# Evacuations of the second group ahead of the norm's broadcast, four plus four low parts on another engine, and one evacuation queued behind the scaling of x, in a gated retention and attention layer

## Chip, cores and metric

The kernel runs on one core of one Trainium2 chip. The metric is device time in microseconds of one execution. The engines are TensorE (PE in the profile, its weight loads PEld), VectorE (DVE), ScalarE (ACT), GpSimd (POOL) and SyncE (SP, which issues the loads).

## The reference

One decoder layer over 256 tokens of width 1024, all in float32. One input projection feeds a retention branch and an attention branch; two gates merge them.

```
def hybrid_layer(x, ln_w, w_in, ret_gn_w, w_ret_o, w_moba_o, w_out):
    h = rmsnorm(x, ln_w)
    proj = jnp.einsum('bsd,de->bse', h, w_in)
    ...
    rq, rk, rv, rg, mq, mk, mv, mg, gr, gm = jnp.split(proj, splits, axis=-1)
    ret = retention(split_heads(rq, RET_HEADS), split_heads(rk, RET_HEADS), split_heads(rv, RET_HEADS))
    ret = head_groupnorm(ret, ret_gn_w).astype(x.dtype) * jax.nn.silu(rg)
    ret = jnp.einsum('bsv,vd->bsd', ret, w_ret_o)
    mo = moba_attention(split_heads(mq, MOBA_HEADS), split_heads(mk, MOBA_HEADS), split_heads(mv, MOBA_HEADS))
    mo = merge_heads(mo) * jax.nn.silu(mg)
    mo = jnp.einsum('bsv,vd->bsd', mo, w_moba_o)
    y = jax.nn.sigmoid(gr) * ret + jax.nn.sigmoid(gm) * mo
    return x + jnp.einsum('bsd,de->bse', y, w_out)
```

A final `rmsnorm` follows. Retention has 4 heads with keys of 128 and values of 256, in two chunks of 128 tokens; the change touches only the first groups of the projection, which feed it.

## The kernel before

Every float32 operand of a product is split into a high part, rounded to the type `float32r`, and a low part, the rest; a product is high times high plus the two mixed terms. A split is one copy on ACT (the high part) and one subtraction on DVE or POOL (the low part).

The weights come in 24 groups of 512 columns, and a group in 4 chunks of 512 KB (`load`, SP's queue, 6 buffers `raw`). `split` (L108, L109) makes `wh` on ACT and `wl` on DVE, 8 buffers each. `stream(g, i)` splits two chunks of group g + 1 and loads two of group g + 2, so the weights run one to two groups ahead. A load waits until DVE has read its `raw` buffer for `wl`.

Groups 0 and 1 are the retention values. They are multiplied with x that the norm has not scaled yet (`x0`, `proj_first`), and the norm's factor `rs` is applied when the two result tiles of a group are evacuated (`evac_n`: `vh` on ACT, L442, and `vl` on DVE, L444). Behind group 1 `x_stats_t` multiplies `rs` with a matrix of ones, which broadcasts it to `rsb` (copied on DVE, L194), and `norm_x(k)` scales the eight slices of x for all later groups: `z` on DVE (L163), the high part of `xs` on ACT (L164), the low part on DVE (L165).

Group 2 (retention queries, `qT`) still multiplies with `x0` and is scaled by `rsb` afterwards (L413). Group 3 (retention keys, `kT`) is the first that needs `xs`. A group of this kind makes four result tiles f = 0 to 3 (`proj_t`), each evacuated by `evac_t`: ACT copies one half, DVE adds the other (`halves`, L392 and L394), and `split_to` makes the high part on ACT (L257) and the low part on POOL (L258). The low parts of the queries are the tile `rqs`, those of the keys lie in `early`. The scores of head 0 (L252 to L254, then L316) stand between groups 3 and 4 in PE's order, and its value product (L336 to L338) between tiles f = 1 and f = 2 of group 4.

The result tiles of all projections share a pool of 4 PSUM buffers (`ps_m`). Groups 0 and 1 use all four; group 2's f = 2 and f = 3 take those of group 1's t = 0 and t = 1, and group 3's f takes that of group 2's f. A tile can begin only when DVE has finished reading the tile before it in its buffer. Each engine works through its own list in order. A scheduler makes the lists when the kernel is built, from the order of the code and its own estimates, so a line moved in the code moves in several lists.

Of the kernel before, what the change touches and what calls it, by code (L numbers as in the profile page):

```python
# [12 lines left out]


# [2 lines left out]

# [6 lines left out]
F32 = mybir.dt.float32  # L24
# [24 lines left out]
def hybrid_kernel(ctx: ExitStack, tc, xT, x, w_in, gn_w, w_ret_o, w_moba_o, w_out, fn_w, decay, out):  # L49
# [110 lines left out]
    def norm_x(k):  # L160
        xk, h, l = xt[:, KT + k * S:KT + (k + 1) * S], xs[:, k, 0], xs[:, k, 1]
        z = wk.tile([P, S], F32, name="z", tag="z", bufs=4)
        nc.vector.scalar_tensor_tensor(z, xk, lnw[:, k:k + 1], rsb, op0=ALU.mult, op1=ALU.mult)  # L163
        nc.scalar.activation(h, z, AF.Copy)  # L164
        nc.vector.tensor_sub(l, z, h.bitcast(F32))  # L165

    def rsqrt(y, a, tmp):

# [28 lines left out]
    def proj_first(g, pair):  # L197

        for k in range(KT):
            for cs in cut(g, k):  # L200
                h, l = (w[g, k // 2][:, k % 2, cs] for w in (wh, wl))
                for t, ps in enumerate(pair):
                    xh, xl = (x0s(k)[:, j, t * P:(t + 1) * P] for j in range(2))
                    nc.tensor.matmul(ps[:, cs], xh, h, start=g > 0 and k == 0, stop=False)  # L204
                    nc.tensor.matmul(ps[:, cs], xh, l, start=False, stop=False)  # L205
                    last = nc.tensor.matmul(ps[:, cs], xl, h, start=False, stop=k == KT - 1)  # L206
        return last
# [45 lines left out]
        nc.tensor.matmul(ps, a[:, 0], b[:, 1], start=False, stop=False)  # L253
        nc.tensor.matmul(ps, a[:, 1], b[:, 0], start=False, stop=True)  # L254

    def split_to(out, a):
        nc.scalar.activation(out[:, 0], a, AF.Copy)  # L257
        nc.gpsimd.tensor_sub(out[:, 1], a, out[:, 0].bitcast(F32))  # L258

    def attn_scores(h):  # L260
        q, k, i = qT[h // 4], kT[h // 4], h % 4
# [125 lines left out]
    def evac_t(g, i, ps):  # L387

        f = (i + 4) if g in (7, 8, 13, 15, 17, 19, 21) else i

        def halves(out, w=1.0):
            nc.scalar.activation(out, ps[:, 1], AF.Copy, scale=w)  # L392
            if w == 1.0:
                nc.vector.tensor_add(out, ps[:, 0], out)  # L394
            else:
                nc.vector.scalar_tensor_tensor(out, ps[:, 0], w, out, op0=ALU.mult, op1=ALU.add)

        def tmp(n):
            return wk.tile([P, S], F32, name=n, tag=n, bufs=4)

        if g in (4, 7):
            q = qT[g // 7][:, i]
            halves(q, 1.0 / math.sqrt(P))
            split_to(qs[g // 7][:, i], q[:, P:])
        elif g in (5, 8):
            k = kT[g // 8][:, i]
            halves(k)
            split_to(ks[g // 8][:, i], k)
        elif g in (2, 3):
            a = (qT if g == 2 else kT)["r"][:, i]  # L410
            halves(a)
            if g == 2:
                nc.vector.tensor_mul(a, a, rsb)  # L413
            split_to((qs if g == 2 else ks)["r"][:, i], a if g == 2 else a[:, :P])
        elif g in (12, 13):
            z, sg = tmp("z"), wk.tile([P, S], F32, name="sg", tag="sg", bufs=2)
            halves(z)
            nc.scalar.activation(sg, z, AF.Sigmoid)
            nc.vector.tensor_mul(z, z, sg)
            nc.vector.tensor_mul(oT[:, f], oT[:, f], z)  # L420
        elif g in (14, 15, 16, 17):
            z = tmp("z")
            halves(z)
            if i % 2 == 0:
                gt = new_v("gt")
                G[g // 16, f], G[g // 16, f + 1] = gt[:, :S], gt[:, S:]
            nc.scalar.activation(G[g // 16, f], z, AF.Sigmoid)
        elif g in (18, 19):
            halves(A[:, f])
            nc.gpsimd.tensor_mul(A[:, f], A[:, f], G[0, f])  # L430
        elif g in (20, 21):
            z = tmp("z")
            halves(z)
            nc.vector.tensor_mul(z, z, G[1, f])
            nc.vector.tensor_add(z, z, A[:, f])
            nc.scalar.activation(yT[:, f, 0], z, AF.Copy)
            nc.vector.tensor_sub(yT[:, f, 1], z, yT[:, f, 0].bitcast(F32))

    def evac_n(g, t, ps):
        def split_v(r1=1.0):  # L440
            h, l = new_v("vh", F32R), new_v("vl", F32R)
            nc.scalar.activation(h, ps, AF.Copy, scale=r1)  # L442
            if g < 2:
                nc.vector.scalar_tensor_tensor(l, ps, r1, h.bitcast(F32), op0=ALU.mult, op1=ALU.subtract)  # L444
            else:
                nc.vector.tensor_sub(l, ps, h.bitcast(F32))
            return h, l

        if g in (6, 9):
            if t == 0:  # L450
                V["m", g // 9] = split_v()
            else:
                v1 = new_v("v1")
                nc.scalar.activation(v1, ps, AF.Copy)
                V["m", g // 9] += (v1,)
        elif g in (0, 1):
            V["r", g] = V.get(("r", g), ()) + (split_v(rs[:, t:t + 1]),)
        elif g in (10, 11):
            nc.scalar.activation(rgate[:, t, (g - 10) * GW:(g - 9) * GW], ps, AF.Copy)
# [9 lines left out]
    def unit(g, i):  # L469

        nonlocal A, yT, rgate
        if i == 0:
            if g == 10:
                rgate = ac.tile([P, NT, D], F32, name="rgate", tag="rgate")
            if g in (2, 4, 7):
                qT["r" if g == 2 else g // 7] = new_qk("qT")
            if g == 2:
                qs["r"] = ac.tile([P, 4, 2, S], F32R, name="rqs", tag="oT")
                early = ac.tile([P, KT + KT * S], F32R, name="early", tag="big8")[:, KT:]
                ks["r"], qs[0] = (early[:, c:c + D].rearrange("p (h a s) -> p h a s", a=2, s=P) for c in (0, D))  # L480
            if g == 5:
                ks[0] = ac.tile([P, 4, 2, S], F32R, name="mk0s", tag="rgate")
            if g == 7:
                qs[1] = ac.tile([P, RET_HEADS * 3 * P], F32R, name="mq1s", tag="dec")[:, :D]
                qs[1] = qs[1].rearrange("p (h a s) -> p h a s", a=2, s=P)
            if g == 8:
                ks[1] = ac.tile([P, KT + KT * S], F32R, name="mk1s", tag="big8")[:, KT:]
                ks[1] = ks[1].rearrange("p (h a s) -> p h a s", a=2, s=S)
            if g in (3, 5, 8):
                kT["r" if g == 3 else g // 8] = new_qk("kT")  # L490
            if g == 18:
                A = ac.tile([P, KT, S], F32, name="A", tag="rgate")
            if g == 20:
                yT = ac.tile([P, KT, 2, S], F32R, name="yT", tag="xs")
        if groups[g][1] == "N":
            evac_n(g, i, proj_n(g, lambda k: xs[:, k], i))
        else:
            if g == 2:
                a = x0s
            elif g < 18:  # L500
                a = lambda k: xs[:, k]
            elif g < 20:
                a = lambda k: rT[k // 2][:, k % 2]
            else:
                a = lambda k: mT[k // 4][:, k % 4]
            for f in (2 * i, 2 * i + 1):
                evac_t(g, f, proj_t(g, a, f))
# [44 lines left out]
    for g in range(2):  # L552
        for i in range(2):
            stream(g, i)
        if g == 0:
            x_stats()
            nc.sync.dma_start(dec, decay)
        pair = [pm.tile([P, GW], F32, name="ps_m", tag="m") for t in range(NT)] if g else ps0
        last = proj_first(g, pair)
        if g:  # L560
            with tc.issue_after(last.ins):
                x_stats_t()
            for k in range(KT):
                norm_x(k)
        for t in range(NT):
            evac_n(g, t, pair[t])
    for g in range(2, NG - 2):
        for i in range(2):
            u = 2 * g + i
            stream(g, i)  # L570
            if u == 38:

                xr = new_v("xr", F32R)
                ir = wk.tile([P, P], F32R, name="ir", tag="p1", bufs=2)
                nc.scalar.activation(ir, ident, AF.Copy)
                nc.scalar.activation(xr[:, :S], xn[:, 1, D - S:], AF.Copy)
                nc.vector.tensor_sub(xr[:, S:], xn[:, 1, D - S:], xr[:, :S].bitcast(F32))
            if u == 40:
                fnw = ac.tile([P, D], F32, name="fnw", tag="qk", bufs=4)
                nc.sync.dma_start(fnw, fn_w.to_broadcast([P, D]))  # L580
                nc.gpsimd.tensor_scalar_mul(fnw, fnw, 2.0)
            for f, a in extra.get(u, []):
                f(*a)
            unit(g, i)
    for c in range(4):
        split(NG - 1, c)

# [89 lines left out]
```

## Time and profile before

| | |
|---|---|
| median of 3 runs | 305.89 us (305.42 to 306.07) |
| the profiled execution's own time | 304.77 us |
| span of that execution in the trace | 302.6 us |
| PE busy, share of the span | 293.8 us, 97% |
| DVE, ACT, POOL busy | 219.7, 192.0, 41.6 us |
| granted clock of PE, mean | 0.996 of full speed |

The profiled execution is one of its own, 1.12 us under the median of the three timed ones; 2.17 us of its time lie outside the span. PE is busy nearly all the time, so what matters are the few places where it waits, and what each of them waits for.

### The profile page before, as it was taken

The numbers are of one execution on the slowest core, as the hardware profiler recorded it, in microseconds if no ns is written. First come the engines' busy times: TensorE is split into PE (matmuls) and PEld (weight loads), VectorE is DVE, ScalarE is ACT, GpSimd is POOL, SyncE is SP. The second block draws the span as 40 slices with busy tenths as digits, with TensorE's granted clock in tenths as the row PEclk, the third lists the DMA queues.
The fourth block names the chain that finished last, engine by engine and source line by source line (L and its number), as shares of the span: only waits on it lengthen the run. The fifth ranks groups of instructions, "written<-read, shape, count | busy, mean of one in ns | idle before, by whom it ended". The sixth has DMA issues, their size and how long they took to land.

```text
span 302.6 us, 4549 instructions
## 1 busy us (share of the span) xinstructions
PE 293.8 (97%) x1628; PEld 253.8 (84%) x1628; DVE 219.7 (73%) x394; ACT 192.0 (63%) x365; POOL 41.6 (14%) x44
## 2 busy tenths in 40 slices
PE   8999999999999999999999999999999999999992
PEld 5788788899888899888888888888888888888891
DVE  3869999867699695884747899557657458899342
ACT  5787777465738676675965857757847626646231
POOL 3000039621200123200000000000000245000000
PEclk9999999999999999999999999999999999999998
DMA  6999659817274462835267184484475486440011
GB/s 195 370 409 410 249 153 341 276 67 223 68 257 128 159 205 76 246 113 198 58 219 233 48 267 147 144 274 126 155 227 179 153 265 215 145 142 1 0 69 69
DMA packets 28966, 55.08 MB, mean 182 GB/s; under 512 B 1936, under 2 KB 3984, under 8 KB 28944
## 3 DMA queue, kind: packets, MB, share of 16 engines
q1 hardware_dynamic: 28624, 54.54, 54.9%
q10 hardware_dynamic: 288, 0.26, 0.2%
q8 instruction: 12, 0.20, 0.2%
q14 instruction: 10, 0.08, 0.1%
q0 software_dynamic: 32, 0.00, 0.0%
HBM read 53.75 MB, written 1.05 MB: 181 GB/s over the span
## 4 chain that ended last, share of the span: by engine, by line
PE 92%; POOL 3%; DVE 2%; ACT 1%; issue 1%; DVEq 0%; POOLq 0%; ACTq 0%
PE ps_m L232 35%; PE ps_m L233 19%; PE ps_m L219 7%; PE ps_m L217 7%; PE ps_m L218 7%; POOL rqs L258 3%; PE ps_m L205 3%; PE ps_m L204 3%; PE ps_m L206 3%; PE ps_s L117 1%; PE ps_t L284 1%; DVE z L163 1%; PE ps_s L263 1%; PE ps_o L303 1%; DVE xs L165 1%
## 5 line engine op out<-in xcount | busy, mean ns | idle before, releaser
L232 PE MATMUL ps_m<-xs,wh 128*128 128x512 f32 x352 | 123.6, 393 | 0.3 <-DVE qT L394 0.3
L109 DVE TENSOR_TENSOR wl<-raw,wh 128x1024 fp32r<-128x1024 f32 x88 | 109.3, 1266 | 11.5 <-ACT wh L108 11.3
L233 PE MATMUL ps_m<-xs,wl 128*128 128x256 f32 x352 | 98.9, 282 | 0.0
L108 ACT ACTIVATE wh<-raw 128x1024 fp32r<-128x1024 f32 x88 | 90.3, 1053 | 7.0 <-PE ps_m L219 2.4
L232 PEld LDWEIGHTS ps_m<-xs,wh 128*128 128x128 f32 x352 | 66.0, 188 | 14.0 <-issue 0.6
L233 PEld LDWEIGHTS ps_m<-xs,wl 128*128 128x128 f32 x352 | 66.5, 189 | 0.2
L217 PE MATMUL ps_m<-wh,xs 128*128 128x512 f32 x64 | 25.5, 398 | 0.0
L218 PE MATMUL ps_m<-wl,xs 128*128 128x512 f32 x64 | 25.3, 395 | 0.0
L219 PE MATMUL ps_m<-wh,xs 128*128 128x512 f32 x64 | 25.3, 395 | 0.0
L430 POOL TENSOR_TENSOR A<-A,gt 128x256 f32<-128x256 f32 x8 | 6.8, 854 | 120.1 <-DVE A L394 120.1
L232 PE MATMUL ps_m<-rT,wh 128*128 128x512 f32 x64 | 22.2, 390 | 0.0
L232 PE MATMUL ps_m<-mT,wh 128*128 128x512 f32 x64 | 22.2, 390 | 0.0
L394 DVE TENSOR_TENSOR z<-ps_m,z 128x256 f32<-128x256 f32 x32 | 13.5, 421 | 11.8 <-ACT z L392 11.7
L392 ACT ACTIVATE z<-ps_m 128x256 f32<-128x256 f32 x32 | 12.1, 379 | 13.1 <-PE ps_m L233 12.9
L233 PE MATMUL ps_m<-rT,wl 128*128 128x256 f32 x64 | 18.0, 282 | 0.0
L233 PE MATMUL ps_m<-mT,wl 128*128 128x256 f32 x64 | 18.0, 282 | 0.0
L258 POOL TENSOR_TENSOR rqs<-qT,rqs 128x256 fp32r<-128x256 f32 x4 | 9.5, 2410 | 39.4 <-ACT rqs L257 39.4
L219 PEld LDWEIGHTS ps_m<-wh,xs 128*128 128x128 f32 x64 | 12.0, 188 | 2.9
L218 PEld LDWEIGHTS ps_m<-wl,xs 128*128 128x128 f32 x64 | 12.0, 188 | 2.5
L217 PEld LDWEIGHTS ps_m<-wh,xs 128*128 128x128 f32 x64 | 12.0, 188 | 2.5
L232 PEld LDWEIGHTS ps_m<-rT,wh 128*128 128x128 f32 x64 | 12.0, 188 | 2.5
L232 PEld LDWEIGHTS ps_m<-mT,wh 128*128 128x128 f32 x64 | 12.0, 188 | 2.5
(183 smaller groups left out, 503.6 us busy)
## 6 DMA issues: line engine op xcount, KB each, us to landing
raw<-in_w_in SPq DMA_DIRECT2D x68, 512.0 KB, 4.7
raw<-in_w_ret_o SPq DMA_DIRECT2D x8, 512.0 KB, 5.5
raw<-in_w_moba_o SPq DMA_DIRECT2D x8, 512.0 KB, 5.4
raw<-in_w_out SPq DMA_DIRECT2D x8, 512.0 KB, 5.1
raw<-in_w_in SPq DMA_DIRECT2D x7, 256.0 KB, 4.8
xn<-in_x SPq DMA_DIRECT2D x2, 512.0 KB, 7.0
xt<-in_xT SPq DMA_DIRECT2D x7, 128.0 KB, 4.1
dec<-in_decay SPq DMA_DIRECT2D x1, 768.0 KB, 9.9
```

The lines of the kernel that those rows point to most:

```text
L108: nc.scalar.activation(h, r, AF.Copy)
L109: nc.vector.tensor_sub(l, r, h.bitcast(F32))
L204: nc.tensor.matmul(ps[:, cs], xh, h, start=g > 0 and k == 0, stop=False)
L205: nc.tensor.matmul(ps[:, cs], xh, l, start=False, stop=False)
L217: nc.tensor.matmul(ps, a(k)[:, 0, sl], h, start=not begun and k == 0, stop=False)
L218: nc.tensor.matmul(ps, a(k)[:, 0, sl], l, start=False, stop=False)
L219: nc.tensor.matmul(ps, a(k)[:, 1, sl], h, start=False, stop=k == KT - 1)
L232: nc.tensor.matmul(ps, h, a(k), start=k == 0, stop=False)
L233: nc.tensor.matmul(ps[:, 0], l, a(k)[:, 0], start=False, stop=k == KT - 1)
L258: nc.gpsimd.tensor_sub(out[:, 1], a, out[:, 0].bitcast(F32))
L392: nc.scalar.activation(out, ps[:, 1], AF.Copy, scale=w)
L394: nc.vector.tensor_add(out, ps[:, 0], out)
```

## The change

Three edits. In the second group, `evac_n` of both tiles stands ahead of `x_stats_t` and `norm_x` in the code; it stood behind. `split_to` takes the engine of the subtraction as an argument, and groups 2 and 3 pass DVE, which moves eight subtractions from POOL: four of 128x256 (`rqs`) and four of 128x128 (`early`, from `kT`). And the first instruction of `norm_x(3)`, the scaling of x's fourth slice on DVE, is kept as `begun`; what unit 4 (group 2's f = 0 and f = 1, with their evacuations) puts on DVE is queued behind it.

```diff
     def norm_x(k):
...
-        nc.vector.scalar_tensor_tensor(z, xk, lnw[:, k:k + 1], rsb, op0=ALU.mult, op1=ALU.mult)
+        ins = nc.vector.scalar_tensor_tensor(z, xk, lnw[:, k:k + 1], rsb, op0=ALU.mult, op1=ALU.mult)
         nc.scalar.activation(h, z, AF.Copy)
         nc.vector.tensor_sub(l, z, h.bitcast(F32))
+        return ins.ins
...
-    def split_to(out, a):
+    def split_to(out, a, eng=nc.gpsimd):
         nc.scalar.activation(out[:, 0], a, AF.Copy)
-        nc.gpsimd.tensor_sub(out[:, 1], a, out[:, 0].bitcast(F32))
+        eng.tensor_sub(out[:, 1], a, out[:, 0].bitcast(F32))
...
-            split_to((qs if g == 2 else ks)["r"][:, i], a if g == 2 else a[:, :P])
+            split_to((qs if g == 2 else ks)["r"][:, i], a if g == 2 else a[:, :P], nc.vector)
...
         last = proj_first(g, pair)
+        for t in range(NT):
+            evac_n(g, t, pair[t])
         if g:
             with tc.issue_after(last.ins):
                 x_stats_t()
-            for k in range(KT):
-                norm_x(k)
-        for t in range(NT):
-            evac_n(g, t, pair[t])
+            begun = [norm_x(k) for k in range(KT)][3]
...
-            unit(g, i)
+            with tc.issue_after(begun) if u == 4 else nullcontext():
+                unit(g, i)
```

The line numbers of the changed kernel are one higher behind the import. DVE's list from the end of group 1 to the evacuation of group 2 (`vl` low parts of the values, `z` and `xs` the norm, `wl` weights) read before:

```order
L194 COPY rsb<-ps_s 128x256
L444 SCALAR_TENSOR_TENSOR vl<-ps_m,rs,vh 128x512
L109 TENSOR_TENSOR wl<-raw,wh 128x1024
L163 SCALAR_TENSOR_TENSOR z<-xt,rsb 128x256 x3
L165 TENSOR_TENSOR xs<-z,xs 128x256 x3
L163 SCALAR_TENSOR_TENSOR z<-xt,rsb 128x256 x3
L165 TENSOR_TENSOR xs<-z,xs 128x256 x3
L163 SCALAR_TENSOR_TENSOR z<-xt,rsb 128x256 x2
L444 SCALAR_TENSOR_TENSOR vl<-ps_m,rs,vh 128x512
L109 TENSOR_TENSOR wl<-raw,wh 128x1024
L165 TENSOR_TENSOR xs<-z,xs 128x256 x2
L109 TENSOR_TENSOR wl<-raw,wh 128x1024
```

and reads now, on the same engine and at the same place:

```order
L445 SCALAR_TENSOR_TENSOR vl<-ps_m,rs,vh 128x512
L109 TENSOR_TENSOR wl<-raw,wh 128x1024
L445 SCALAR_TENSOR_TENSOR vl<-ps_m,rs,vh 128x512
L195 COPY rsb<-ps_s 128x256
L163 SCALAR_TENSOR_TENSOR z<-xt,rsb 128x256 x4
L109 TENSOR_TENSOR wl<-raw,wh 128x1024
L165 TENSOR_TENSOR xs<-z,xs 128x256 x4
L163 SCALAR_TENSOR_TENSOR z<-xt,rsb 128x256 x3
L165 TENSOR_TENSOR xs<-z,xs 128x256 x2
L163 SCALAR_TENSOR_TENSOR z<-xt,rsb 128x256
L109 TENSOR_TENSOR wl<-raw,wh 128x1024
L165 TENSOR_TENSOR xs<-z,xs 128x256 x2
```

Both `vl` stand at the front, the second no longer behind all eight `z`; the sum of instructions is the same. The first evacuation of group 2 (`qT`) follows directly behind each of the two pieces.

What follows on DVE, from that evacuation on (`rqs` and `early` are the subtractions that POOL had), reads now:

```order
L395 TENSOR_TENSOR qT<-ps_m,qT 128x256 x2
L414 TENSOR_TENSOR qT<-qT,rsb 128x256 x2
L109 TENSOR_TENSOR wl<-raw,wh 128x1024
L259 TENSOR_TENSOR rqs<-qT,rqs 128x256 x2
L109 TENSOR_TENSOR wl<-raw,wh 128x1024
L395 TENSOR_TENSOR qT<-ps_m,qT 128x256 x2
L414 TENSOR_TENSOR qT<-qT,rsb 128x256 x2
L109 TENSOR_TENSOR wl<-raw,wh 128x1024
L259 TENSOR_TENSOR rqs<-qT,rqs 128x256 x2
```

The `rqs` rows are new here and stand between two `wl`; before, the two `wl` followed each other. Later in the same list `early` stands twice behind the `wl` that follows `kT`'s first evacuations.

Before, POOL's list at that place read

```order
L258 TENSOR_TENSOR rqs<-qT,rqs 128x256 x4
L258 TENSOR_TENSOR early<-kT,early 128x128 x4
L258 TENSOR_TENSOR early<-qT,early 128x128 x4
L258 TENSOR_TENSOR mk0s<-kT,mk0s 128x256 x4
```

and the first two of these rows are gone from it now; the attention's low parts (`early` from group 4's `qT`, then `mk0s`) stay.

## Rows read from the trace of the kernel before

**Rows 1.** Waits, PE alone, whole run: waiter, releaser, us in total, times, longest

```profile
PE ps_s L254 <- POOL early L258: 0.8, 1, 0.8
PE ps_m L232 <- DVE vl L444: 0.6, 1, 0.6
PE ps_m L232 <- DVE qT L394: 0.3, 1, 0.3
```

**Rows 2.** Busy time by stretch: us, each engine's busy us (instructions), clock, DMA share, GB/s

```profile
37.68:53.50 15.82, 14.70 (x83) 12.61 (x83) 15.46 (x23) 12.16 (x23) 11.02 (x6) 1.00 0.77 249
...
62.00:298.00 236.00, 234.69 (x1331) 205.39 (x1330) 168.68 (x307) 147.24 (x288) 23.31 (x23) 1.00 0.48 152
```

**Rows 3.** Timeline, PE, 36 to 58 us: start, us, line, out<-in, [idle <- releaser]

```profile
37.68 0.50 PE L232 MATMUL ps_m<-x,wh 128*128 128x512 f32 x1 [0.59 <-DVE vl L444]
...
41.04 0.47 PE L232 MATMUL ps_m<-xs,wh 128*128 128x512 f32 x1 [0.32 <-DVE qT L394]
...
52.25 0.28 PE L252 MATMUL ps_s<-rqs,early 128*128 128x256 f32 x1
52.37 0.28 PE L253 MATMUL ps_s<-rqs,early 128*128 128x256 f32 x1
53.46 0.39 PE L254 MATMUL ps_s<-rqs,early 128*128 128x256 f32 x1 [0.80 <-POOL early L258]
```

**Rows 4.** Timeline, DVE, 26 to 58 us, columns as above

```profile
28.77 0.42 DVE L194 COPY rsb<-ps_s 128x256 f32<-128x256 f32 x1 [0.42 <-PE ps_s L192]
29.11 0.74 DVE L444 SCALAR_TENSOR_TENSOR vl<-ps_m,rs,vh 128x512 fp32r<-128x512 f32 x1
29.77 1.22 DVE L109 TENSOR_TENSOR wl<-raw,wh 128x1024 fp32r<-128x1024 f32 x1
30.90 1.27 DVE L163 SCALAR_TENSOR_TENSOR z<-xt,rsb 128x256 f32<-128x256 f32 x3
...
33.21 0.76 DVE L165 TENSOR_TENSOR xs<-z,xs 128x256 fp32r<-128x256 f32 x2 [0.70 <-ACT xs L164]
...
36.09 0.88 DVE L163 SCALAR_TENSOR_TENSOR z<-xt,rsb 128x256 f32<-128x256 f32 x2
36.88 0.75 DVE L444 SCALAR_TENSOR_TENSOR vl<-ps_m,rs,vh 128x512 fp32r<-128x512 f32 x1
...
40.48 0.75 DVE L394 TENSOR_TENSOR qT<-ps_m,qT 128x256 f32<-128x256 f32 x2
...
51.40 3.08 DVE L109 TENSOR_TENSOR wl<-raw,wh 128x1024 fp32r<-128x1024 f32 x2 [0.36 <-ACT wh L108]
...
56.34 0.82 DVE L322 TENSOR_TENSOR il<-inn,ih 128x384 fp32r<-128x384 f32 x1
```

**Rows 5.** Timeline, ACT, 26 to 58 us, columns as above

```profile
27.63 0.69 ACT L442 ACTIVATE vh<-ps_m,rs 128x512 fp32r<-128x512 f32 x1 [1.19 <-PE ps_m L206]
28.21 1.05 ACT L108 ACTIVATE wh<-raw 128x1024 fp32r<-128x1024 f32 x1
...
32.49 0.39 ACT L392 ACTIVATE qT<-ps_m 128x256 f32<-128x256 f32 x1 [0.66 <-PE ps_m L233]
...
34.63 1.02 ACT L164 ACTIVATE xs<-z 128x256 fp32r<-128x256 f32 x3
...
44.99 1.06 ACT L108 ACTIVATE wh<-raw 128x1024 fp32r<-128x1024 f32 x1 [0.90 <-DMA raw<-in_w_in]
```

**Rows 6.** Instructions of line L258 on POOL: duration ns min/median/max, first and last start

```profile
L258 POOL TENSOR_TENSOR rqs<-qT,rqs x4: 736/2626/3650, 42.5 to 51.3; 128x256 fp32r<-128x256 f32 x4
...
L258 POOL TENSOR_TENSOR early<-kT,early x4: 455/1438/1496, 52.0 to 55.2; 128x128 fp32r<-128x128 f32 x4
L258 POOL TENSOR_TENSOR early<-qT,early x4: 460/748/1306, 58.1 to 69.5; 128x128 fp32r<-128x128 f32 x4
```

**Rows 7.** DMA issues by line: count, KB each, median us from issue to landing

```profile
raw<-in_w_in SPq DMA_DIRECT2D x68, 512.0 KB, 4.7
...
dec<-in_decay SPq DMA_DIRECT2D x1, 768.0 KB, 9.9
```

More of the change, by code (lines that the diff above doesn't have):

```diff
@@ L15 @@
 import math
-from contextlib import ExitStack
+from contextlib import ExitStack, nullcontext
 import concourse.bass as bass
```

## Prediction

> **What bounds the kernel now.** I read the waits of PE first. Behind the first microseconds they name three and no more [rows 1]: 0.8 us for a low part from POOL, 0.6 us for a `vl` on DVE, 0.3 us for an evacuation of `qT` on DVE. The stretch from 62 us to 298 us shows PE busy for 234.69 of 236.00 us at a granted clock of 1.00, with DVE at 168.68 us, 71% [rows 2]. So the kernel is bound by PE's own work, and all that an edit of the order can win lies between 37 and 54 us. There DVE is the full engine: 15.46 of 15.82 us busy [rows 2].
>
> PE's timeline puts the three waits in place [rows 3]. At 37.68 group 2's last tile f = 3 begins, 0.59 us late, because its PSUM buffer is group 1's second value tile, and `vl` of that tile ran only at 36.88 [rows 4]; its high part on ACT had long been made. At 41.04 group 3's first tile begins, 0.32 us late, behind `qT`'s addition at 40.48. At 53.46 the third product of head 0's scores begins. The two before it started 0.12 us apart, at 52.25 and 52.37, so its own slot was 52.49 and it is 0.97 us late, where the wait is listed with 0.80. It waited for POOL: four `rqs` subtractions with a median of 2.63 us each stand in POOL's list ahead of the first `early`, which takes up to 1.50 us [rows 6].
>
> The three are not to be added blindly: all of DVE's work between 28.8 and 41 us must be done before the tile at 41.04 can begin, so a wait removed at 37.68 comes back at 41.04 unless DVE itself gets there earlier.
>
> **The change part by part.** *Evacuations first.* Nothing is added on DVE: copy, two `vl`, three `wl`, eight `z`, eight `xs`, in another order. What counts is the time at which the last of them is done, so I walk the new list with durations of the old rows. From one start to the next a `vl` takes 0.66 us (29.11 to 29.77), a `wl` 1.13 (29.77 to 30.90), the copy and all other 128x256 forms 0.34, a `z` 0.40 (36.09 to 36.88 for two) [rows 4]. On ACT a `wh` takes 1.05, less the tenth by which neighbours overlap, and three `xs` 1.02 [rows 5].
>
> The high part of the first value tile ends at 28.32 [rows 5], so its `vl` starts at 28.4, into the gap in which DVE waited 0.42 us for the broadcast [rows 4]. The `wl` behind it needs the `wh` that ends at 29.26: 29.3. The second `vl` starts at 30.4, the copy at 31.1, four `z` at 31.55 to 33.1. The next `wl` needs a `wh` that on ACT now stands behind `qT`'s first evacuation; its tile's last products move up two places in PE's list, about 0.35 us, so that evacuation comes at 32.15 and not 32.49 [rows 5], the `wh` ends at 33.5, and DVE waits 0.4. Then `wl` to 34.65, four `xs` to 36.0 with no wait, since ACT has had a `wl` of time to make the high parts (this is where 0.70 us were lost before, at 33.21). Three `z` to 37.2, two `xs` from 37.25, a `z`, a `wl` from 38.3, two `xs` from 39.45, and `qT`'s addition at 40.1 instead of 40.48. Its result is there 0.42 + 0.04 us later, and PE begins group 3 at 40.6 instead of 41.04: **-0.4 us**. The wait at 37.68 is gone (that `vl` is done at 31.2), but PE arrives at 39.75 at the end of its tile and waits 0.8 us at group 3 in place of 0.3. Bounds: nothing, if ACT is later than the walk by 0.4; 0.91, both waits, if DVE did not hold PE at all, which would need 0.8 us less work in its list.
>
> *The binding behind the fourth slice.* In the new list `qT`'s addition stands behind all eight slices, as it did before. It costs and brings nothing beyond the walk.
>
> *Eight low parts on DVE.* POOL loses eight subtractions with medians of 2.63 and 1.44 us [rows 6]. DVE gets 4 subtractions of 128x256 at 0.34 and 4 of 128x128. The trace of before has no such 128x128 on DVE; between nothing and the 0.34 of twice the width I take 0.20. Sum 2.1 us on an engine that is 98% busy there, so something must give way. I walk on from 40.1: two additions, two scalings by `rsb`, `wl` from 41.45, two `rqs` from 42.6 (their high parts are done on ACT by 42.2), the `wl` of group 3's last chunk from 43.25 to 44.5. Before, that `wl` was done 0.3 us earlier. PE gets to the product that needs it at 44.6: a margin of 0.1 us. Then the second pair of additions and scalings, a `wl`, two `rqs`, a `wl`, the two additions of `kT` from 48.7, a `wl`, and the first `early` at 50.5, ready at 50.8. PE, 0.4 us earlier than before, wants it at 52.49 - 0.4 = 52.1. So the wait of 0.97 us is gone with 1.3 us to spare: **-0.97 us**. Bounds: 0 if DVE were 2.3 us later than walked, 0.97 if not.
>
> What is late next? Behind that, DVE has two `wl`, two `early`, two additions, a `wl` and a `wl` more before the low part `il` of head 0's scores, which the walk has at 57.7, done at 58.3; before it started at 56.34. PE wants it for the value product at 58.35. This margin is nil, so I charge **+0.15 us**: between 0 and the 0.6 us of the next paragraph. Behind 62 us DVE is 71% busy [rows 2], so nothing is handed on from there.
>
> A stretch on DVE is the open price. The two `wl` at 51.40 took 3.08 us, where two of 1.22 take 2.35, while POOL worked on its `early`; `il` took 0.82, where the 0.42 of 256 columns and the 0.74 of 512 put 384 columns at 0.58 [rows 4]. And the same POOL subtraction takes 0.74 to 3.65 us [rows 6]. So the two engines hold each other up. The Trainium skill, in "SBUF — State Buffer", section "SBUF: two separate sides", says that a DVE operation with two SBUF inputs and a POOL operation lock one pair of ports for a whole instruction. These rows agree with that. By the rule alone DVE would get back the 0.7 us by which the two `wl` were stretched, the 0.15 us above would be nothing, and the sum 1.35 us; but what POOL keeps would still collide.
>
> **The sum.** -0.4 - 0.97 + 0.15 = -1.2 us against the profiled execution's 304.77 us (302.6 of span and 2.17 around it), so 303.55. That execution stood 1.12 us under the median of the runs. The metric is that median, so I forecast 305.89 - 1.2 = **304.7 us**, 0.4% faster. A difference of less than 0.2%, 0.6 us, cannot be told from none for this kernel (its three runs lie 0.65 apart).
>
> **The rivals.**
>
> *The collisions stay.* POOL's `early` of group 4 starts when ACT has made its high part at about 57.1, during the `wl` and the `il` that PE is about to need. Price, by the stretches above: 0.36 for a `wl` and 0.24 for `il`, 0.6 us: 305.3 us. For it: the stretched rows of before. Against: the `wl` at 29.77, with POOL idle, and most of the others are alike at 1.22. Of the rules of the Trainium skill the port lock named above would give this outcome.
>
> *The wait comes back on DVE.* DVE walks with nearly no gap from 28 to 59 us, on margins of 0.1 us at 44.6 and nil at 58.35. Before, its list lost 0.70 and 0.36 us to ACT [rows 4]. If it loses another 0.6 to 1.4 us, PE waits for `wl` or `il` for just that long: 305.3 to 306.1, about 305.8 us, no change. For it: 98% of busy time and eight more instructions. Against: the walk already holds three waits of DVE for ACT, 1.1 us, as much as was lost before.
>
> *All three waits vanish.* If `qT`'s addition came 0.8 us before the walk, the sum would be 0.91 + 0.97 = 1.88: 304.0 us. Against it stands DVE's list, in which no work was taken away ahead of that addition.
>
> *Slower, by one load.* The second `early` on DVE needs a high part that on ACT now stands behind the first `wh` of group 5, and that needs its load, issued when `wl` frees the buffer at 42.7. DVE's `wl` for group 4's last chunk is queued behind that `early`; PE wants it at 54.7. With 2.9 us of `wh`, high part, `early` and `wl` in between, a load that lands behind 51.8 stops PE us for us, and behind 53.7 it eats the gain and 0.6 us more: 306.6 us. The median landing takes 4.7 us, so 47.4; the longest, of 768 KB, 9.9 [rows 7]; 11 would be needed. One load did hold ACT for 0.90 us, at 44.99 [rows 5].
>
> **How the numbers follow.** Chances: the forecast (304.3 to 305.1) 0.50; collisions 0.14; back on DVE 0.18; all vanish 0.08; slower 0.10. Faster by over 0.6 us: 0.50 + 0.08 + half of the collisions = 0.65. Slower: 0.10. The rest, 0.25, is the same. The range goes from 303.9 (all three waits) to 305.9 (a gain used up on DVE) and leaves out the slow case and little more.
>
> **What would show it.** Right: no wait of PE for POOL near 52 us, and none at f = 3 of group 2; one wait of 0.6 to 1.0 us at group 3's first tile, which starts at 40.4 to 40.8; `vl` of group 1 at 28.4 and 30.4 on DVE. Wrong: a wait of PE for `wl` near 44 us, for `early` near 52, or for `il` near 58 us of over 0.3 us; or group 3 starting at 41.0 or later.

## The result, and the profile after

The changed kernel takes 304.44 us (median of 9 runs, 303.53 to 305.6); the kernel before, on the same chip, 306.05 us (9 runs, 305.42 to 306.76). The ratio is 0.9947, with an interval of 0.9928 to 0.9967: 0.5% faster. The forecast was 304.7 us, in a range of 303.9 to 305.9.

The profiled execution of the changed kernel is the slowest of its nine (305.6 us), and that of before was lower than any of the timed ones, so that the two spans, 302.7 and 302.6 us, show no gain at all. The list of PE's waits, in total, times and the longest, shows where the disturbance lies:

```profile
PE ps_s L117 <- DVE warm L114: 1.2, 1, 1.2
PE ps_m L233 <- ACT qT L393: 0.8, 1, 0.8
PE ps_m L206 <- DVE wl L109: 0.5, 1, 0.5
```

The three waits of [rows 1] are gone, and one of 0.8 us stands in their place. The 0.5 us for `wl` lie at 18.8 us, in group 1, which the change doesn't touch; all runs below, the repeat of before too, have 0.5 to 1.1 us of such waits for the first weights, and only the first execution of before has none. So I count all times from the norm's broadcast, the first product behind group 1. It begins at 28.13 us before, at 29.66 here, 1.53 us later:

```profile
29.66 0.38 PE L193 MATMUL ps_s<-ident,rs 128*128 128x128 f32 x2
```

From there to the end of the span are 274.50 us before and 273.03 us now: **-1.47 us** (the ends are taken from the trace to hundredths; the views give the span to tenths). A second execution of each gives 274.52 and 273.04, so this difference repeats within 0.02 us. The stretch ahead of it does not repeat: the broadcast begins at 28.13 and 28.75 us in the two executions of before and at 29.66 and 29.16 us in those of the changed kernel. Up to there PE, DVE, ACT and POOL work through the same instructions in the same order in every run of this document. The medians speak against a longer stretch in the changed kernel: they differ by 1.61 us, and by 1.74 in the repeat, no less than 1.47.

PE's timeline at the places of [rows 3]:

```profile
42.17 0.47 PE L233 MATMUL ps_m<-xs,wh 128*128 128x512 f32 x1 [0.79 <-ACT qT L393]
...
53.38 0.28 PE L253 MATMUL ps_s<-rqs,early 128*128 128x256 f32 x1
53.50 0.28 PE L254 MATMUL ps_s<-rqs,early 128*128 128x256 f32 x1
53.62 0.28 PE L255 MATMUL ps_s<-rqs,early 128*128 128x256 f32 x1
53.74 0.38 PE L317 MATMUL ps_s<-qT,kT 128*128 128x128 f32 x2
```

Group 3 begins 12.51 us behind the broadcast (12.91 before). The three score products stand 0.12 us apart with no wait, and the one behind them begins at 24.08 us behind the broadcast (25.55 before). These are the two pieces of the gain, 0.40 and 1.07 us.

DVE's timeline, to be held against [rows 4] with 1.53 us taken off:

```profile
29.89 0.74 DVE L445 SCALAR_TENSOR_TENSOR vl<-ps_m,rs,vh 128x512 fp32r<-128x512 f32 x1
30.83 1.23 DVE L109 TENSOR_TENSOR wl<-raw,wh 128x1024 fp32r<-128x1024 f32 x1 [0.19 <-ACT wh L108]
31.97 0.75 DVE L445 SCALAR_TENSOR_TENSOR vl<-ps_m,rs,vh 128x512 fp32r<-128x512 f32 x1
32.63 0.42 DVE L195 COPY rsb<-ps_s 128x256 f32<-128x256 f32 x1
33.08 1.67 DVE L163 SCALAR_TENSOR_TENSOR z<-xt,rsb 128x256 f32<-128x256 f32 x4
35.04 1.23 DVE L109 TENSOR_TENSOR wl<-raw,wh 128x1024 fp32r<-128x1024 f32 x1 [0.28 <-ACT wh L108]
...
41.61 0.75 DVE L395 TENSOR_TENSOR qT<-ps_m,qT 128x256 f32<-128x256 f32 x2
...
44.08 0.75 DVE L259 TENSOR_TENSOR rqs<-qT,rqs 128x256 fp32r<-128x256 f32 x2
...
51.96 0.28 DVE L259 TENSOR_TENSOR early<-kT,early 128x128 fp32r<-128x128 f32 x1
52.72 0.29 DVE L259 TENSOR_TENSOR early<-kT,early 128x128 fp32r<-128x128 f32 x1 [0.48 <-ACT early L258]
...
59.34 0.55 DVE L323 TENSOR_TENSOR il<-inn,ih 128x384 fp32r<-128x384 f32 x1
```

The `vl` stand at 28.36 and 30.44 on the clock of before (walked: 28.4 and 30.4), the addition at 40.08 (40.1), the first `rqs` at 42.55 (42.6), `early` at 50.43 (50.5), `il` at 57.81 (57.7). Up to the keys the list waits for ACT only where the walk had it wait (0.19 and 0.28 us). The wait at 42.17 is listed under an ACT copy of `qT`; the one that ends just then, at 42.05, is the fourth tile's, and those of the first two tiles were done by 37.45. What the buffer waited for is DVE's first addition: begun at 41.61, it takes 0.42 us, and PE starts 0.14 us behind its end, the same distance as in [rows 3, 4].

The two stretches of [rows 2], the first one moved by the 1.5 us to the same work. The columns are PE, PEld, DVE, ACT and POOL busy with counts, the granted clock, the DMA share and GB/s:

```profile
39.21:55.03 15.82, 15.03 (x89) 13.10 (x89) 15.34 (x29) 11.97 (x23) 0.00 (x0) 1.00 0.64 196
62.00:298.00 236.00, 234.76 (x1332) 205.46 (x1330) 169.11 (x309) 147.73 (x288) 23.33 (x24) 1.00 0.49 155
```

POOL is empty there, and DVE, with more instructions than before, is busy for 15.34 of 15.82 us, no more than the 15.46 of before.

### The profile page after: what moved, and what is told of

Same layout as the page of the kernel before. It is cut to its first block, busy times and chain, and to the rows that moved or that the text cites. A ratio compares the mean times of both kernels' runs of the same rounds, so it can differ in the third digit from the quotient of the medians.

```text
span 302.7 us, 4547 instructions
## 1 busy us (share of the span) xinstructions
PE 294.2 (97%) x1628; PEld 253.1 (84%) x1628; DVE 220.7 (73%) x402; ACT 191.5 (63%) x365; POOL 28.6 (9%) x36
## 4 chain that ended last, share of the span: by engine, by line
PE 89%; DMA 4%; ACT 3%; SPq 1%; DVE 1%; issue 1%; DVEq 0%; ACTq 0%
PE ps_m L233 37%; PE ps_m L234 19%; PE ps_m L218 7%; PE ps_m L220 7%; PE ps_m L219 7%; DMA raw<-in_w_in 2%; ACT wh L108 2%; DMA xt<-in_xT 2%; PE ps_m L206 1%; PE ps_m L207 1%; PE ps_m L205 1%; PE ps_t L285 1%; SPq L87 1%; ACT xs L164 1%; PE ps_s L264 1%
## 5 line engine op out<-in xcount | busy, mean ns | idle before, releaser
L206 PE MATMUL ps_m<-wl,x 128*128 128x512 f32 (+1 forms) x34 | 13.7, 404 | 0.5 <-DVE wl L109 0.5
```

## Experiments

Each run is given by its ratio to the kernel before in the same batch, with the interval, and by four distances from the broadcast on PE: the start of group 3, the end of head 0's scores (its first `qT,kT` product), its value product, and the end of the span.

| kernel | median us | ratio | group 3 | scores | value product | span's end |
|---|---|---|---|---|---|---|
| before | 306.05 | | 12.91 | 25.55 | 31.32 | 274.50 |
| before, again | 305.55 | 0.9996 [0.9979, 1.0013] | 12.92 | 25.56 | 31.34 | 274.52 |
| changed | 304.44 | 0.9947 [0.9928, 0.9967] | 12.51 | 24.08 | 29.86 | 273.03 |
| changed, again | 304.19 | 0.9939 [0.9927, 0.9952] | 12.51 | 24.08 | 29.86 | 273.04 |
| lows_dve | 304.55 | 0.9954 [0.9938, 0.9971] | 12.91 | 24.48 | 30.26 | 273.43 |
| evac_bind | 305.47 | 0.9992 [0.9977, 1.0008] | 12.52 | 25.16 | 30.94 | 274.11 |
| evac_first | 307.69 | 1.0078 [1.0055, 1.0102] | 11.57 | 26.79 | 34.08 | 277.26 |
| no_bind | 304.62 | 0.9968 [0.9953, 0.9982] | 11.57 | 23.91 | 30.69 | 274.09 |
| keys_only | 304.38 | 0.9956 [0.9941, 0.9972] | 12.51 | 24.07 | 29.85 | 273.03 |
| queries_only | 304.14 | 0.9940 [0.9922, 0.9959] | 12.52 | 24.12 | 29.90 | 273.08 |
| keys_late6 | 304.10 | 0.9941 [0.9927, 0.9956] | 11.57 | 23.72 | 29.50 | 272.67 |
| late6_all | 304.59 | 0.9950 [0.9930, 0.9970] | 11.57 | 23.60 | 29.84 | 273.42 |

**Only the low parts on DVE** (lows_dve): the kernel before with `split_to`'s new argument and its call for groups 2 and 3, and nothing else of the change.

```diff
-            split_to((qs if g == 2 else ks)["r"][:, i], a if g == 2 else a[:, :P])
+            split_to((qs if g == 2 else ks)["r"][:, i], a if g == 2 else a[:, :P], nc.vector)
```

> Only the eight low parts move to DVE; evacuations and binding as before. My theory (two separate waits: DVE's order gives 0.4 us at group 3, POOL's queue gives 0.97 us at head 0's scores): the waits at group 2's f = 3 (0.6 us) and at group 3 (0.3 us) stay, the one of 0.8 us on POOL is gone; the stretch from the broadcast to the first product of group 4 shrinks by 0.9 to 1.0 us, the time by 0.8 to 1.0 us, ratio 0.997. Rival (what DVE takes over comes back as waits on DVE, and the change's gain is the evacuations'): stretch shorter by under 0.4 us, ratio 0.999 or more, with a wait of PE for wl near 44 us or il near 58 us.

PE's waits in it:

```profile
PE ps_m L232 <- DVE vl L444: 0.6, 1, 0.6
PE ps_m L232 <- DVE qT L394: 0.3, 1, 0.3
```

Two of the three waits of [rows 1] stay as they were, and POOL's is gone. The scores end 1.07 us earlier, the whole size of the second piece (expected: 0.9 to 1.0). So the low parts alone bring 1.08 of the 1.47 us, and DVE carries eight more instructions without being late for PE.

**Evacuations and binding, the low parts left on POOL** (evac_bind): the changed kernel, and

```diff
-            split_to((qs if g == 2 else ks)["r"][:, i], a if g == 2 else a[:, :P], nc.vector)
+            split_to((qs if g == 2 else ks)["r"][:, i], a if g == 2 else a[:, :P])
```

> The changed kernel with all eight low parts back on POOL: evacuations first and the binding alone. The first products of group 3 and the scores are counted from the norm's broadcast on PE, since the stretch before it varies by itself. Theory (the change is a gain at group 3 by the evacuations, which the score's wait for POOL swallows unless the low parts leave it): group 3 begins 12.5 us behind the broadcast, as in the changed kernel (12.9 before); POOL's four subtractions of the queries take 10 to 11 us beside DVE and its list ends no earlier than before, so the last product of head 0's scores is at 25 to 26.5 us (25.55 before, 24.08 in the changed kernel), PE waits 1 to 2.5 us for POOL at it, and the ratio to the kernel before is 0.998 to 1.003; if that wait is as long as in the variant with the evacuations alone (2.8 us), the clock may fall to half behind it and the ratio is up to 1.006. Rival (the parts add up): POOL follows the queries, which come 0.4 us earlier, the score keeps 0.4 us, and the ratio is 0.9985.

POOL's timeline, and the product that waits for it:

```profile
42.88 9.75 POOL L259 TENSOR_TENSOR rqs<-qT,rqs 128x256 fp32r<-128x256 f32 x4 [39.77 <-ACT rqs L258]
52.59 4.77 POOL L259 TENSOR_TENSOR early<-kT,early 128x128 fp32r<-128x128 f32 x4
```

```profile
54.08 0.38 PE L255 MATMUL ps_s<-rqs,early 128*128 128x256 f32 x1 [0.82 <-POOL early L259]
```

Here my theory of a longer wait (1 to 2.5 us) fell and the rival held. POOL's `early` begins 23.45 us behind the broadcast, 0.39 earlier than before, as the queries do; the wait stays as long as it was and the 0.39 us are kept to the scores (25.16 against 25.55). From the broadcast to the end it is 0.39 us shorter; the ratio alone could not tell that from nothing. With lows_dve (1.08 us) the sum is 1.47 us, and the whole change has 1.47: the parts add up.

**Only the evacuations first** (evac_first): the kernel before with the moved block, neither binding nor low parts.

```diff
+        for t in range(NT):
+            evac_n(g, t, pair[t])
         if g:
...
-        for t in range(NT):
-            evac_n(g, t, pair[t])
```

> Only the evacuations of the second group move ahead; low parts on POOL, no binding. In DVE's list the first addition of qT now stands right behind the broadcast's copy, at 31.5 us, where its ACT half is ready only at 32.5 us. My theory: DVE loses 1 us there, the wait at group 2's f = 3 goes, group 3 begins earlier but waits for wl, and the wait on POOL at head 0's scores grows from 0.8 to about 1.2 us, since POOL's first input comes no earlier: nothing is won, ratio 0.999 to 1.001. Rival (the evacuations are the larger part of the gain): ratio 0.997 or less with the score's wait unchanged.

Neither expectation held: this one is slower than before, by 0.8%, and the wait is 2.79 us and not 1.2. DVE's timeline behind the broadcast's copy:

```profile
32.56 0.41 DVE L194 COPY rsb<-ps_s 128x256 f32<-128x256 f32 x1
34.03 0.42 DVE L394 TENSOR_TENSOR qT<-ps_m,qT 128x256 f32<-128x256 f32 x1 [1.06 <-ACT qT L392]
34.37 1.66 DVE L163 SCALAR_TENSOR_TENSOR z<-xt,rsb 128x256 f32<-128x256 f32 x4
```

Without the binding the scheduler puts `qT`'s first addition right behind the copy, where DVE waits 1.06 us for ACT's half with all eight `z` queued behind it. That addition is early, so group 3 begins at 11.57; the rest of DVE's list is not, and POOL's subtractions gain nothing by it:

```profile
43.86 10.80 POOL L258 TENSOR_TENSOR rqs<-qT,rqs 128x256 fp32r<-128x256 f32 x4 [40.75 <-ACT rqs L257]
54.62 2.68 POOL L258 TENSOR_TENSOR early<-kT,early 128x128 fp32r<-128x128 f32 x4
```

They begin 14.27 us behind the broadcast (14.35 before, 13.74 in evac_bind), and the four `rqs` take 10.80 us (9.52 before, 9.75 in evac_bind). Most of that is the fourth, 1.71 us in place of 0.74: before, it began in the 0.36 us in which DVE waited for a `wh` (51.40 in [rows 4]), and here DVE has no such gap. So the first `early` is 1.19 us later than before, while PE comes earlier. PE waits at the scores, and then runs slowly:

```profile
53.04 0.28 PE L253 MATMUL ps_s<-rqs,early 128*128 128x256 f32 x1
56.11 0.48 PE L254 MATMUL ps_s<-rqs,early 128*128 128x256 f32 x1 [2.79 <-POOL early L258]
...
57.45 0.63 PE L232 MATMUL ps_m<-xs,wh 128*128 128x512 f32 x1
...
59.86 0.39 PE L232 MATMUL ps_m<-xs,wh 128*128 128x512 f32 x1
```

The windows of the same stretch (columns as above) give the granted clock:

```profile
54.00:56.00 2.00, 0.00 (x0) 0.00 (x0) 2.00 (x3) 1.92 (x4) 2.00 (x2) 1.00 1.04 368
56.00:57.00 1.00, 0.89 (x4) 0.89 (x5) 0.07 (x1) 0.31 (x1) 1.00 (x4) 0.62 1.02 385
57.00:58.00 1.00, 1.00 (x5) 0.81 (x4) 0.94 (x2) 0.00 (x0) 0.30 (x1) 0.50 0.85 174
58.00:59.00 1.00, 1.00 (x5) 0.90 (x4) 0.74 (x1) 0.00 (x0) 0.00 (x0) 0.50 0.90 330
60.00:61.00 1.00, 1.00 (x8) 0.88 (x7) 0.00 (x0) 0.00 (x0) 0.00 (x0) 1.00 0.68 129
```

Behind 2.79 us without a product PE gets half its clock, the lower of its two levels (1.2 GHz), for some 3 us. The two tiles behind the scores take 7.29 us (34.08 less 26.79) where they take 5.77 before, so 1.5 us are lost to the clock on top of 1.24 at the scores. Two of the six runs have a span of 306.8 us, the profiled one among them, and four 305.4 to 305.6; the gap is about what the clock cost here. Two of these four have a mean granted clock of 0.997 and 0.998, which leaves no room for such a stretch (it takes half a per cent off the mean); for the other two, at 0.991 and 0.992, it isn't shown whether they kept the clock.

**The change without its binding** (no_bind).

```diff
-            with tc.issue_after(begun) if u == 4 else nullcontext():
-                unit(g, i)
+            unit(g, i)
```

> The changed kernel without the binding. The prediction said that the binding costs and brings nothing. Theory now, from DVE's list: without it DVE waits about 1 us for qT's first addition ahead of all eight z, all of DVE's list comes 0.7 to 1 us later, and PE waits for wl in group 3 (0.4 us or more, twice) and for il near 59 us (0.4 to 0.8 us): slower than the changed kernel by 0.8 to 1.1 us, faster than before by 0.2 to 0.5 us, ratio 0.998 to 0.9995. Rival (as predicted, the binding does nothing): ratio as the changed kernel's, 0.995.

DVE's list begins as in evac_first, group 3 begins 0.94 us earlier than in the changed kernel, and the scores end 0.17 us earlier. All of it is lost before the value product, which is 0.83 us later; a further 0.23 us are lost behind its start, where its third product stands 1.64 us behind the first (0.60 in the changed kernel). Rows on PE, ACT (two) and DVE (two):

```profile
60.27 0.38 PE L337 MATMUL ps_o<-vh,ih 128*128 128x256 f32 x1 [1.07 <-ACT ih L322]
```

```profile
56.27 1.06 ACT L108 ACTIVATE wh<-raw 128x1024 fp32r<-128x1024 f32 x1 [1.69 <-DMA raw<-in_w_in]
57.23 0.49 ACT L258 ACTIVATE early<-kT 128x128 fp32r<-128x128 f32 x2
```

```profile
57.56 0.49 DVE L259 TENSOR_TENSOR early<-kT,early 128x128 fp32r<-128x128 f32 x2 [1.48 <-ACT early L258]
...
59.10 0.55 DVE L319 TENSOR_TENSOR inn<-ps_s,dec 128x384 f32<-128x384 f32 x1
```

A weight's load is late for ACT; the last two high parts of the keys are queued behind its `wh`; DVE's list stands still at their low parts, with a `wl` and `inn` queued behind, which the value product needs. This is the kind of chain that the prediction named as the slower rival (there with the second `early` and a weight of group 4), at a smaller price. In the changed kernel ACT's `wh` at that place (55.07) waits for no load and the third `early` stands ahead of it, so that only the fourth is behind. The load is issued when DVE's `wl` has freed its buffer, 21.43 us behind the broadcast against 20.65, so 0.78 us of its lateness come from DVE's list. But it also takes 5.18 us to land, against 4.49 and 4.54 in the two executions of the changed kernel, and that this is the edit's doing isn't shown. In these executions the binding is worth 1.06 us to the end of the span (274.09 against 273.03), of which up to 0.7 us may be that landing's chance; in time it is 0.2 to 0.3% (0.9968 against 0.9947 and 0.9939, with intervals that overlap or nearly touch). Of the expectation the size in the trace held; the ratio is below its range, and the two waits for `wl` and `il` were one for `wl` (0.4 us) and one for `ih`. Without the low parts the binding is worth 3.1 us (evac_first against evac_bind), half of that by the clock, and in time 0.9%.

**Which low parts matter** (keys_only, queries_only): the changed kernel with the queries' four, or the keys' four, back on POOL.

```diff
+            split_to((qs if g == 2 else ks)["r"][:, i], a if g == 2 else a[:, :P], nc.gpsimd if g == 2 else nc.vector)
...
+            split_to((qs if g == 2 else ks)["r"][:, i], a if g == 2 else a[:, :P], nc.vector if g == 2 else nc.gpsimd)
```

> The changed kernel with the four low parts of the queries (128x256) back on POOL; only the four of the keys (128x128) on DVE. It tells POOL's queue from the count of instructions on DVE. My theory: what made the first key's low part late was its place behind four query low parts in POOL's list; taken from that list alone, the score's wait is gone, and DVE has 1.3 us less to do, so nothing is late behind it: stretch from the broadcast to group 4 as in the changed kernel, ratio 0.995 to 0.996. Rival (POOL and DVE hold each other up over a shared port, so that POOL's four subtractions beside DVE's list must cost DVE): wl of 1.5 to 2 us on DVE between 43 and 52 us, stretch longer than the changed kernel's by 0.4 us or more, ratio 0.997.

> The counterpart of the run with the keys' low parts alone on DVE: here the four of the queries (128x256) are on DVE and the four of the keys (128x128) stay on POOL. If the cause of the score's wait is the place in POOL's list, the first key's low part now stands first there and starts as soon as its high part is there, 21.5 us behind the broadcast, takes 0.5 to 1.5 us, and is ready before PE wants it at 23.9: no wait, the last product of head 0's scores at 24.1 us behind the broadcast, ratio 0.995 to 0.996. If POOL's slowness beside DVE is the cause whatever its place, a wait of 0.3 us or more for POOL is seen there.

POOL's timeline in keys_only, and then in queries_only:

```profile
43.23 11.13 POOL L259 TENSOR_TENSOR rqs<-qT,rqs 128x256 fp32r<-128x256 f32 x4 [40.12 <-ACT rqs L258]
```

```profile
50.47 3.91 POOL L259 TENSOR_TENSOR early<-kT,early 128x128 fp32r<-128x128 f32 x3 [47.36 <-ACT early L258]
```

Either half takes the whole wait away (scores at 24.07 and 24.12, 24.08 with both). What cost PE 0.97 us was that four long subtractions and the `early` stood in one list. POOL's work itself, 11.13 us beside DVE, does PE no harm when nothing urgent is queued behind it: the `wl` of 1.5 to 2 us that the rival in keys_only asks for are not there, the longest takes 1.40.

**Is the wait at group 3 a loss of its own?** (keys_late6, late6_all) The last two slices of x are scaled behind unit 4, so that `qT`'s first additions stand ahead of them on DVE; keys_late6 has the queries' low parts on POOL besides, as keys_only.

```diff
-            begun = [norm_x(k) for k in range(KT)][3]
+            begun = [norm_x(k) for k in range(6)][3]
...
+            if u == 4:
+                for k in range(6, KT):
+                    norm_x(k)
```

> A version that should beat the changed kernel: only the keys' low parts on DVE, and the scaling of x's last two slices behind unit 4, so that qT's first additions stand 1.7 us earlier in DVE's list. My theory (DVE's list ahead of qT's addition sets the start of group 3, now the one wait left, 0.8 us): group 3 begins 0.8 us earlier, 11.7 us behind the broadcast, but its seventh slice now waits for xs or wl for 0.2 to 0.4 us, and il may cost 0.4: net -0.1 to -0.6 us against the changed kernel. Rival (the wait left is PE's own hand-over with ACT, as the list of waits names it): group 3 at 12.5 us as before, no gain.

> The changed kernel with the last two slices of x scaled behind unit 4, so that the additions of the queries' first tiles stand earlier on DVE, and all eight low parts on DVE. Theory (DVE's list is full, so what leaves the place ahead of group 3 is missing later): group 3 begins 11.6 us behind the broadcast without a wait (12.5 in the changed kernel), but a weight's low part is 0.4 to 1.0 us late behind it, so that the last product of head 0's scores is at 23.7 to 24.6 us and the ratio to the kernel before is 0.993 to 0.996. Rival (the wait at group 3 was a loss of its own): the score is at 23.2, and the ratio is 0.992.

Both begin group 3 at 11.57 with no wait, which confirms that DVE's addition is what it waits for in the changed kernel. Of the 0.94 us won there, keys_late6 keeps 0.36 at the end of the span. PE's next wait in it, and DVE's row ahead of that:

```profile
46.19 0.38 PE L234 MATMUL ps_m<-xs,wl 128*128 128x256 f32 x1 [0.40 <-DVE wl L109]
```

```profile
43.47 1.53 DVE L165 TENSOR_TENSOR xs<-z,xs 128x256 fp32r<-128x256 f32 x2 [0.24 <-ACT xs L164]
```

The two `xs` took 1.53 us where they take 0.76 elsewhere, while POOL ran two `rqs` (41.97 to 44.72). late6_all has no POOL work there and ends the scores at 23.60, 0.48 us ahead of the changed kernel, without the wait that I expected for `wl`; but then it meets the same late load as no_bind (ACT's `wh` at 55.25 waits 0.87 us, PE 0.31 for `ih`). Its value product is level with the changed kernel's, breaks off behind two products as in no_bind, and at the end of the span it is 0.39 us behind. keys_late6 is the best of all by the trace; in time, 304.10 against 304.19 us on the same chip, it can't be told from the changed kernel.

> The kernel before once more, unchanged. If the first stage is chance, its broadcast is not at 28.13 us again but somewhere from 28 to 30 us, with the same 25.55 us behind it; if the changed order makes that stage longer, it is at 28.1 us again.

> The changed kernel once more, unchanged. The traces so far agree to 0.02 us in what lies behind the broadcast (before: 25.55 us from the broadcast to the last product of head 0's scores, changed: 24.08), but the broadcast itself begins at 28.13 to 29.66 us, in a stage that no edit touches. If that stage is chance, this run has 24.1 again with a broadcast anywhere from 27.5 to 30 us, and a ratio of 0.994 to 0.997. If the change made the stage longer, the broadcast is at 29.5 us or later again.

These two gave the repeats in the table: all four distances from the broadcast agree within 0.02 us. The broadcast itself is at 28.75 us in the first and at 29.16 us in the second: each moved by 0.5 to 0.6 us against its own kernel's first execution, towards the other's. So that stage is not fixed; two executions of each can't show by themselves whether its mean moved, and for that the medians stand.

## Why the prediction was right, point by point

**Evacuations first, -0.4 us.** Right in size and place: group 3 at 12.51 instead of 12.91. One term was too short: the walk lets PE begin 0.04 us behind the addition's end, where the rows of before have 0.14 (40.90 to 41.04); it is small enough not to show. The walk through DVE's new list held within 0.1 us up to the keys, because every duration in it came from a row of the same engine and the places where ACT holds DVE were put into it.

**The low parts, -0.97 us.** Right: lows_dve alone shows it. Measured are 1.07; the further 0.10 us is the product behind the wait, which before took 0.22 us to the next one (53.46 to 53.68) where it takes 0.12 in a row. The 128x128 subtraction takes 0.28 us on DVE, and 0.21 from its start to the next one (55.53 to 55.74); I had put 0.20.

**+0.15 us at `il`.** The time was right and the charge was not. `il` ends at 59.89. In PE's order of before, the product that needs it is the third of the value product, 0.24 us behind the first:

```profile
59.45 0.28 PE L336 MATMUL ps_o<-vh,ih 128*128 128x256 f32 x1
59.57 0.28 PE L337 MATMUL ps_o<-vl,ih 128*128 128x256 f32 x1
59.69 0.28 PE L338 MATMUL ps_o<-vh,il 128*128 128x256 f32 x1
```

In that order it would be due at 59.76 now, so PE would have waited about as long as charged. PE's order is another now:

```profile
59.52 0.28 PE L337 MATMUL ps_o<-vh,ih 128*128 128x256 f32 x1
59.64 0.28 PE L338 MATMUL ps_o<-vl,ih 128*128 128x256 f32 x1
59.76 0.28 PE L253 MATMUL ps_s<-rqs,early 128*128 128x256 f32 x1
59.88 0.28 PE L254 MATMUL ps_s<-rqs,early 128*128 128x256 f32 x1
60.00 0.28 PE L255 MATMUL ps_s<-rqs,early 128*128 128x256 f32 x1
60.12 0.28 PE L339 MATMUL ps_o<-vh,il 128*128 128x256 f32 x1
```

The scheduler put three score products of head 1, which stood behind the whole value product, ahead of the one that needs `il`. I read the new order on DVE and ACT and not this piece of PE's; that the charge fell away was luck. The margin of 0.1 us at group 3's last chunk held as well.

**"It costs and brings nothing beyond the walk"**, of the binding, is the step that failed. It was right that the list with the binding behaves as walked; but I compared it with the list of before, not with what the moved block makes of that list without the binding. There `qT`'s first addition goes ahead of the norm, and the binding is worth 1.06 us in the traces, 0.2 to 0.3% in time. The forecast did not suffer, since the change has the binding. A forecast of the moved block alone, made in my way, would have missed a loss of 0.8%.

**The sum.** -1.2 us was forecast and the trace has -1.47: the 0.15 us that were charged and didn't come, and the 0.10 not counted. The medians differ by 1.61 us here and by 1.74 in the repeat, a further 0.1 to 0.3, within what the first 29 us move by themselves (0.6 us between two executions of before). Correcting the sum to the median of before and not to the profiled execution was right; the profiled spans alone would have shown no gain.

**The rivals.** The collisions did not decide: POOL's first `early` of group 4 starts at 58.80 and takes 2.54 us, while DVE's `wl` and `il` beside it take 1.22 and 0.55, as alone. So it was POOL that stood still. The wait did not come back on DVE, which lost 0.48 us more to ACT than the walk held, at 52.72, and had the time. Nor did all three waits vanish. The late load came in no_bind and late6_all and not in the changed kernel.

## What to carry to other kernels

When a low-priority list and an urgent instruction share an engine, moving either away can be enough, as here; count the list ahead of the urgent one, not the engine's busy share. When a scheduler makes the lists, cost each edit against the list that it makes by itself: an edit that looks idle beside the old order can be what holds the new one together, and the order of the engine that bounds the kernel is to be read as closely as that of the others. And where a kernel's first microseconds move by more than the change does, count from a fixed instruction behind them.

## What the runs showed of the hardware

**The clock after a wait.** In the profiled execution of evac_first a wait of 2.79 us cost 1.5 us more by half a clock behind it, while waits of 0.8 to 1.1 us show a granted clock of 1.00 behind them in the stretches read here. So a wait's price need not be its length.

**POOL beside DVE.** The four 128x256 subtractions take 9.52, 9.75, 10.80 and 11.13 us on POOL beside a busy DVE (before, evac_bind, evac_first, keys_only), 2.4 to 2.8 each, and 0.42 each on DVE; the same subtraction takes 0.74 us on POOL at its shortest [rows 6]. That shortest one is the fourth, and what it takes goes with DVE's gaps: 0.74 and 0.73 us where it begins while DVE waits 0.35 to 0.36 us for ACT (before, evac_bind), 1.71 and 1.72 where DVE has no gap (evac_first, keys_only). DVE pays less: 1.53 in place of 0.76 us for two `xs`, and 0.82 in place of 0.55 for an `il` beside POOL's `early` (before, no_bind, late6_all). The Trainium skill, in "SBUF — State Buffer", section "SBUF: two separate sides", has it that of a POOL instruction and a DVE instruction with two SBUF inputs, whichever starts first gets the shared ports for the whole instruction and the other stands still. The rows agree, with most of the cost on POOL as long as DVE's list has no gaps.
